# Scans of the last groups: x rows loaded inside the by-tile projection, row products one scan step later

## The chip, the cores and the metric

The kernel runs on one core of a Trainium2 chip. A core has five engines that run side by side, each through its own list of instructions, strictly in the order of that list: TensorE (PE, matrix products, with its weight loads shown as PEld), VectorE (DVE), ScalarE (ACT), GpSimd (POOL) and SyncE (SP), which here only issues DMA transfers. Engines wait for each other, and for transfers, on semaphores. An instruction that waits holds up all that stands behind it on its engine, and that goes for the transfers in SP's list too.

The metric is the time of one execution in microseconds (us), the median of several runs. A run with the profiler on leaves a trace, from which the profile is made; its times are counted from the start of the span.

## The reference

One inference step of a trunk with two layers over 1024 prompt tokens (one sequence) and 64 sample tokens (8 sequences of 8): a Mamba-2 SSD layer, then a layer of causal pooling. Each layer normalises x, modulates it, applies its branch and adds the result to x through a gate. Cut to the SSD branch, which is where the change lies:

```python
D_MODEL, D_INNER, N_HEADS, HEAD_DIM, N_GROUPS, D_STATE, CHUNK = 1024, 2048, 32, 64, 8, 128, 128

def ssd_branch(h, conv_prev, ssm_prev, w_in, conv_w, conv_b, dt_bias, a_log, d_skip, norm_g, w_out):
    zxbcdt = h @ w_in                                  # z, x/B/C and dt of every token
    conv = conv_b + sum(xp[:, k:k + L] * conv_w[k] for k in range(CONV_WIDTH))
    xbc_act = silu(conv)
    ...
    y, new_ssm = ssd_scan(xs, dt, A, Bm, Cm, ssm_prev) # chunks of 128 tokens, state passed on
    y = (y + d_skip[:, None] * xs).reshape(b, L, D_INNER)
    gated = (y * silu(z)).reshape(b, L, N_GROUPS, D_INNER // N_GROUPS)
    gated = gated * rsqrt(mean(gated * gated, axis=-1, keepdims=True) + EPS)
    gated = gated.reshape(b, L, D_INNER) * norm_g
    return gated @ w_out, new_conv, new_ssm
```

The eight groups are independent in the scan. The normalisation of `gated` goes over the 256 channels of one group, so a group's rows are final as soon as its own scan is done, and `gated @ w_out` can be added up over groups. x then becomes x + (1 + gate) * out.

## The kernel before

**Tiles.** Activations lie with channels on the 128 partitions and all 1088 tokens (1024 + 64) along the row. The tokens are worked in three pieces `CH` of 368, 368 and 352. Every matrix product is made in float32 out of halves: an activation is split into a high part (`gh`, `hh`, a rounding copy on ACT) and the rest (`gl`, `hl`, a subtraction on DVE), a weight likewise into `wh` and `wl`, and three matmuls (L184 high by high, L185 low activation, L186 low weight) replace one.

**The SSD layer.** `ssd_layer` goes through the eight groups. `scan_group(g)` is a generator that does one group's scan in 11 steps and leaves two more (the mean square with its rsqrt and the row products) as `rest`, which is run during the next group's scan. Beside each step the table `FILL` takes one to five pieces of other work out of `beside()`: first the projections of groups 1, 2, 3, 4 and 6, then the out-projection in parts. This other work is there to keep TensorE busy, since a scan is a chain of small operations over all engines.

**The projection by tile.** The last projection tile of all (group 6, fourth tile) doesn't run piece by piece but over the eight input tiles k one after the other, holding three accumulators (`ps`), so that each input tile's two buffers are given back as soon as it was used. Between its steps `next(self.prep)` loads and splits the rows for the first part of the out-projection: `op_stage` fetches a row tile `gr` from DRAM (`gyd`, L756), `op_split` makes `gh` (ACT, L761) and `gl` (DVE, L762). A part has four row tiles, and `op_part_load` has five steps. At the end the accumulators are evicted into `raw` by ACT (`proj_evict`, L424 and L426).

**The out-projection.** `op_units(p)` adds part p (four row tiles, of two groups) to all eight x tiles. `load_x` fetches an x tile (L1587), two tiles ahead (`XA = 2`), `op_evict` adds the product to it (DVE, L803, L806, L808), and the result goes to DRAM (`x1d`, L1612) until the next part. The very first tile (`op_first`, L786 to L791) does all the `gh` matmuls of all three pieces before any of `gl`.

**A scan's own operations**, as far as the text speaks of them. For each of eight chunks of 128 tokens: a load of decays `acb` from DRAM (L539; three tiles take turns), from which ACT makes the mask factors `M` (L571, L572), `ea` (L555) and `cd` (L591); transposes (`tr`, L563 and L566); a copy `Bt` (L583); a state sum `S` on PE (L605); the new state `h` (DVE, L610 and L614) and the rows `y` on PE (L626 from `M`, L630 from the state). For the samples: states `h0` are loaded (L528), read by PE (`Z`, L645), updated (DVE, L684) and stored (`hsT`, L686). When all rows are there they are multiplied by `z` (L721), squared (ACT, L722), summed (L723) and averaged with a matmul against ones (L727); the root goes through DRAM (`rsd`, L732) and comes back spread over all partitions (`rs`, L735). The row products then are two operations of DVE, each followed by its store:

```python
        for q in range(2):
            nc.vector.scalar_tensor_tensor(out=xs[q], in0=xs[q], scalar=..., in1=rst, op0=ALU.mult, op1=ALU.mult)  # L739
            if g < 7:
                nc.sync.dma_start(self.gyd[2 * g + q], xs[q])                                                     # L742
```

**Buffers.** `x`, `gr`, `gh`, `gl`, `h0`, `z`, `rs` and `xbc` all come out of one list of 30 buffers (`Slots`), handed out first in, first out: the n-th request gets the buffer that was given back n-th. So a request that moves ahead of another changes which buffer each later one gets, and what each must wait for.

**What sets the order.** The code above fixes which operations there are and what depends on what. The order of the instructions on each engine is then worked out by a scheduler with costs of its own, so a line that moves in the source may move other instructions too.

Of the kernel before, what the change touches and what calls it, by code (L numbers as in the profile page):

```python
# [28 lines left out]
XA = 2  # L29
# [70 lines left out]
class Build:  # L100
# [289 lines left out]
    def proj_group(self, G):  # L390

        for ii in range(4):
            w = self.stream_next()
            raw = self.proj_begin(G, ii)
            if (G["g"], ii) == (BESIDE[-1], 3):

                ps = [self.mm_tile() for _ in CH]
                for k in range(8):
                    for c, j in ((0, k), (1, k), (2, 0), (2, k)) if k == 1 else ((0, k), (1, k), (2, k))[:3 if k else 2]:
                        self.mm1(ps[c], w, j, self.hn[j], CH[c], j == 0, j == 7)  # L400
                    for j in (0, 1) if k == 1 else (k,) if k else ():
                        self.slots.free(*self.hn[j])
                    if k:
                        next(self.prep, None)
                    if k < 7:
                        yield
                for c in range(3):
                    self.proj_evict(G, ii, raw, ps[c], c, False)
                yield
                self.late = lambda: self.proj_end(G, ii, raw, True)  # L410
                return
            ada = self.ada_do(self.ada_plan[G["g"], ii]) if (G["g"], ii) in self.ada_plan else iter(())
            for c in range(3):
                ps = self.mm_tile()
                self.mm3(ps, w, self.hn, CH[c])
                self.proj_evict(G, ii, raw, ps, c)
                if c:
                    next(ada, None)
                yield
# [1101 lines left out]
    def ssd_layer(self):  # L1521
        nc, sl = self.nc, self.slots
        T, rest = {0: self.G[0]["out"]}, iter(())
        self.x = [None] * 8
        self.acts = [[] for _ in PARTS]
        self.prep = self.op_part_load(0, self.acts[0])
        self.fill = self.beside(T)
        for g in range(8):
            sc = self.scan_group(g, T[g])
            for i, n in enumerate(FILL[g]):  # L1530
                next(sc)
                for j in range(n):
                    next(self.fill)
                    if i in (0, 3) and j == 0:
                        next(rest, None)
                if i == 8 and g + 1 in self.G:
                    T[g + 1] = [sl.get("xbc") for _ in range(4)]
                    for t, d in zip(T[g + 1], self.xbd[g + 1]):
                        nc.sync.dma_start(t, d)
            rest = sc  # L1540
        self.prep = self.op_part_load(3, self.acts[3])
        self.out_unit()
        next(rest)
        for _ in range(2):
            next(self.fill)
        self.out_unit()
        for _ in rest:
            pass
# [39 lines left out]

    def op_units(self, p):

        for d in range(XA):
            self.load_x(p, d)
        for d in range(8):
            if d > 7:
                if (p, d) in self.ada_late:
                    for _ in self.ada_do(self.ada_late[p, d]):
                        pass
                    yield None
                continue
            self.load_x(p, d + XA)  # L1600
            if d % 2 == 0:
                ws = self.stream_pair()
            blk = self.ada_do(self.ada_late[p, d]) if (p, d) in self.ada_late else iter(())
            if p + d == 0:
                yield from self.op_first(0, self.x, d, ws[0], self.acts[p])
            for i, ch in enumerate(CH if p + d else ()):
                ins = self.op_unit(0, self.x, d, ws[d % 2], self.acts[p], ch)
                if i != 1:
                    next(blk, None)
                yield ins  # L1610
            if p < 2:
                self.nc.sync.dma_start(self.x1d[d], self.x[d])  # L1612
                self.slots.free(self.x[d])
# [264 lines left out]
```

## Time and profile before

| | |
|---|---|
| median of 3 runs | 1607.52 us (1605.69 to 1610.42) |
| the profiled execution | 1610.37 us, its span 1608.6 us |
| granted TensorE clock, mean | 0.996 |
| PE busy | 1579.8 us, 98% of the span |
| DVE, ACT, POOL busy | 1295.1, 792.3, 506.4 us |
| PE idle in the span | 28.8 us (1608.6 less 1579.8) |

The profiled execution is 2.85 us above the median of the three runs, so a sum made on its times is carried over to the median as a difference. TensorE is busy almost all of the time; what an edit of order can give or take is its idle time, which the profile names with the instruction that came late ("PE y L630 <- DVE h L610" reads: a matmul of line 630 waited for a DVE operation of line 610 on the tile h). In a timeline row the first number is the start, the second the duration, and a bracket at the end tells how long the engine had been idle before it and for whom. A row with "x3" stands for three instructions of that kind in a run. The changed lines act in the scans of groups 5, 6 and 7, some 690 to 930 us into the span.

### The profile page before, as it was taken

The numbers are of one execution on the slowest core, as the hardware profiler recorded it, in microseconds if no ns is written. First come the engines' busy times: TensorE is split into PE (matmuls) and PEld (weight loads), VectorE is DVE, ScalarE is ACT, GpSimd is POOL, SyncE is SP. The second block draws the span as 40 slices with busy tenths as digits, with TensorE's granted clock in tenths as the row PEclk, the third lists the DMA queues.
The fourth block names the chain that finished last, engine by engine and source line by source line (L and its number), as shares of the span: only waits on it lengthen the run. The fifth ranks groups of instructions, "written<-read, shape, count | busy, mean of one in ns | idle before, by whom it ended". The sixth has DMA issues, their size and how long they took to land.

```text
span 1608.6 us, 30632 instructions
## 1 busy us (share of the span) xinstructions
PE 1579.8 (98%) x11916; PEld 1506.0 (94%) x11916; DVE 1295.1 (81%) x2152; ACT 792.3 (49%) x1512; POOL 506.4 (31%) x558
## 2 busy tenths in 40 slices
PE   8999999999999999999999999999999999999997
PEld 6899999998888889888898899999999999999997
DVE  6974879778888888788889867998889776677886
ACT  6663344457676666674555437532232233333364
POOL 0133556512231313131212232275666630000241
PEclk9999999999999999999999999999999999999999
DMA  9422232355645554768998532132333279465783
GB/s 351 165 100 100 78 111 83 110 180 158 197 156 172 165 188 145 235 226 282 304 336 300 207 131 78 58 143 102 115 112 110 106 255 350 139 173 177 161 175 120
DMA packets 122305, 275.58 MB, mean 171 GB/s; under 512 B 18192, under 2 KB 59312, under 8 KB 122160
## 3 DMA queue, kind: packets, MB, share of 16 engines
q1 hardware_dynamic: 118128, 260.90, 47.2%
q0 software_dynamic: 4032, 12.72, 4.5%
q8 instruction: 94, 1.54, 0.4%
q14 instruction: 51, 0.42, 0.1%
HBM read 201.12 MB, written 70.23 MB: 169 GB/s over the span
## 4 chain that ended last, share of the span: by engine, by line
PE 79%; DVE 8%; DMA 5%; issue 4%; ACT 3%; POOL 1%; SPq 0%; DVEq 0%; ACTq 0%; POOLq 0%
PE st L1032 10%; PE st L1030 10%; PE st L1031 10%; PE mm L184 10%; PE mm L185 9%; PE mm L186 9%; PE op L1247 2%; PE op L1248 2%; PE op L1246 2%; PE y L626 2%; PE S L605 2%; PE y L630 2%; PE am L255 1%; PE tr L566 1%; DMA acb<-acd 1%
## 5 line engine op out<-in xcount | busy, mean ns | idle before, releaser
L1030 PE MATMUL st<-hh,w 128*128 128x272 f32 x832 | 240.3, 289 | 0.8 <-ACT w L176 0.8
L1032 PE MATMUL st<-hh,w 128*128 128x272 f32 x832 | 240.4, 289 | 0.4 <-DVE w L178 0.4
L1031 PE MATMUL st<-hl,w 128*128 128x272 f32 x832 | 240.0, 288 | 0.0
L1030 PE MATMUL st<-t,w 128*128 128x272 f32 x624 | 179.6, 288 | 0.0
L1032 PE MATMUL st<-t,w 128*128 128x272 f32 x624 | 179.5, 288 | 0.0
L1031 PE MATMUL st<-t,w 128*128 128x272 f32 x624 | 179.2, 287 | 0.0
L184 PE MATMUL mm<-hh,wh 128*128 128x368 f32 (+1 forms) x528 | 178.2, 338 | 0.0
L185 PE MATMUL mm<-hl,wh 128*128 128x368 f32 (+1 forms) x528 | 173.6, 329 | 0.0
L186 PE MATMUL mm<-hh,wl 128*128 128x368 f32 (+1 forms) x528 | 173.3, 328 | 0.0
L1030 PEld LDWEIGHTS st<-hh,w 128*128 128x128 f32 x832 | 156.8, 188 | 1.3 <-ACT w L176 1.3
L1032 PEld LDWEIGHTS st<-hh,w 128*128 128x128 f32 x832 | 156.4, 188 | 0.9 <-DVE w L178 0.9
L1031 PEld LDWEIGHTS st<-hl,w 128*128 128x128 f32 x832 | 156.7, 188 | 0.0
L613 POOL TENSOR_TENSOR hd<-h,cd 128x256 f32<-128x256 f32 x56 | 46.8, 836 | 322.6 <-DVE h L614 165.2
L176 ACT ACTIVATE w<-wr 128x512 fp32r<-128x512 f32 x104 | 64.9, 629 | 166.3 <-PE st L1032 137.4
L1247 PE MATMUL op<-b,w 128*128 128x272 f32 x448 | 128.9, 288 | 0.7 <-DVE b L1176 0.7
L1246 PE MATMUL op<-b,w 128*128 128x272 f32 x448 | 129.5, 289 | 0.0
L1248 PE MATMUL op<-b,w 128*128 128x272 f32 x448 | 128.9, 288 | 0.0
L184 PE MATMUL mm<-gh,wh 128*128 128x368 f32 (+1 forms) x372 | 125.6, 339 | 2.0 <-DVE x L803 1.9
L186 PE MATMUL mm<-gh,wl 128*128 128x368 f32 (+1 forms) x372 | 122.3, 329 | 0.0
L185 PE MATMUL mm<-gl,wh 128*128 128x368 f32 (+1 forms) x372 | 121.9, 328 | 0.1
L1030 PEld LDWEIGHTS st<-t,w 128*128 128x128 f32 x624 | 117.6, 189 | 0.1
L1032 PEld LDWEIGHTS st<-t,w 128*128 128x128 f32 x624 | 117.3, 188 | 0.0
(307 smaller groups left out, 4564.8 us busy)
## 6 DMA issues: line engine op xcount, KB each, us to landing
wr<-win SPq DMA_DIRECT2D x48, 512.0 KB, 6.0
acb<-acd SPq DMA_DIRECT2D x64, 256.0 KB, 4.6
wr<-pin SPq DMA_DIRECT2D x32, 512.0 KB, 3.8
wr<-pout SPq DMA_DIRECT2D x28, 512.0 KB, 4.7
x<-x1d SPq DMA_DIRECT2D x24, 544.0 KB, 5.7
x1d<-x SPq DMA_DIRECT2D x22, 544.0 KB, 4.7
wr<-pout POOLq DMA_DIRECT2D x20, 512.0 KB, 5.9
x<-xT SPq DMA_DIRECT2D x16, 544.0 KB, 7.3
```

Source lines behind the costliest of these rows:

```text
L176: self.nc.scalar.activation(hi, src, AF.Copy)
L184: nc.tensor.matmul(ps[:, :n], hi[:, k, :], ah[:, a:a + n], start=first, stop=False)
L185: nc.tensor.matmul(ps[:, :n], hi[:, k, :], al[:, a:a + n], start=False, stop=False)
L186: nc.tensor.matmul(ps[:, :n], lo[:, k, :], ah[:, a:a + n], start=False, stop=last)
L605: nc.tensor.matmul(S[:, 256 * i:256 * i + 256], Bt, xde.rearrange("p r q -> p (r q)"), start=True, stop=True)
L613: nc.gpsimd.tensor_tensor(out=hd, in0=h[-1], in1=cd.unsqueeze(2).to_broadcast([P, 4, 64]), op=ALU.mult)
L1030: nc.tensor.matmul(ps[c][:, :QUART], hi[:, k], xh[:, t], start=(k == 0), stop=False)
L1031: nc.tensor.matmul(ps[c][:, :QUART], hi[:, k], xl[:, t], start=False, stop=False)
L1032: nc.tensor.matmul(ps[c][:, :QUART], lo[:, k], xh[:, t], start=False, stop=(k == 3))
L1246: nc.tensor.matmul(ps[:, :QUART], hi[:, k], xh, start=k == 0, stop=False)
L1247: nc.tensor.matmul(ps[:, :QUART], hi[:, k], xl, start=False, stop=False)
L1248: nc.tensor.matmul(ps[:, :QUART], lo[:, k], xh, start=False, stop=k == 7)
```

## The change

```diff
@@ proj_group: the by-tile projection of the last tile
                         self.mm1(ps[c], w, j, self.hn[j], CH[c], j == 0, j == 7)
                     for j in (0, 1) if k == 1 else (k,) if k else ():
                         self.slots.free(*self.hn[j])
-                    if k:
+                    if k in (4, 5):
+                        self.load_x(0, k - 4)
+                    if 0 < k < 7:
                         next(self.prep, None)
                     if k < 7:
                         yield
                 for c in range(3):
                     self.proj_evict(G, ii, raw, ps[c], c, False)
+                next(self.prep, None)
                 yield
@@ ssd_layer
                 for j in range(n):
                     next(self.fill)
-                    if i in (0, 3) and j == 0:
+                    if i in (0, 3 + (g > 4)) and j == 0:
                         next(rest, None)
@@ op_units
-        for d in range(XA):
+        for d in range(XA if p else 0):
             self.load_x(p, d)
```

Three things are edited. First, the x tiles 0 and 1 of the out-projection's first part are requested at the steps k = 4 and 5 of the by-tile projection, each ahead of that step's gate load and split, and no more at the head of `op_units`. Second, the last call of `prep` in the projection stands behind its evictions. Third, in the scans of groups 5, 6 and 7 the second piece of `rest`, the row products of the group before (4, 5 and 6), is run at scan step 4 instead of 3.

The number and kinds of the instructions stay as they were. In the changed kernel the lines behind the first hunk are numbered three higher (L424 is L427, L739 is L742, L761 is L764, and so on). The order of the instructions differs only in the stretch named above. Three places:

ACT, at the end of the by-tile projection. `gh` are the gate halves of the first out-projection part, each from its loaded row `gr`; `raw<-mm` is the projection's eviction; `z<-xbc` is the square of the rows. The numbers behind a name count the tiles. Before:

```order
L761 ACTIVATE gh_139_8404<-gr_135_8387 128x1088
L761 ACTIVATE gh_142_8442<-gr_138_8402 128x1088
L362 ACTIVATE raw1106_8108<-raw1136_8306 128x1112
L761 ACTIVATE gh_144_8455<-gr_141_8440 128x1088
L424 ACTIVATE raw1145_8352<-mm1146_8355 128x368
L424 ACTIVATE raw1145_8352<-mm1147_8356 128x368
L141 ACTIVATE wh1153_8487<-wr1144_8350 128x1024
L424 ACTIVATE raw1145_8352<-mm1148_8357 128x288
L426 ACTIVATE raw1145_8352<-mm1148_8357 128x8x8
L722 ACTIVATE z_128_8214<-xbc_121_7586 128x1088
L359 ACTIVATE raw1200_8738<-raw1145_8352,cwh_263 128x1112
```

And after:

```order
L764 ACTIVATE gh_139_8404<-gr_135_8387 128x1088
L764 ACTIVATE gh_143_8444<-gr_138_8402 128x1088
L362 ACTIVATE raw1106_8108<-raw1136_8306 128x1112
L427 ACTIVATE raw1145_8352<-mm1146_8355 128x368
L427 ACTIVATE raw1145_8352<-mm1147_8356 128x368
L141 ACTIVATE wh1153_8487<-wr1144_8350 128x1024
L427 ACTIVATE raw1145_8352<-mm1148_8357 128x288
L429 ACTIVATE raw1145_8352<-mm1148_8357 128x8x8
L725 ACTIVATE z_128_8214<-xbc_121_7586 128x1088
L764 ACTIVATE gh_146_8459<-gr_142_8442 128x1088
L359 ACTIVATE raw1200_8738<-raw1145_8352,cwh_263 128x1112
```

The fourth gate half (gh_144 before, gh_146 after, of the same row) moved from ahead of the evictions to behind the square; its new buffer is the one that the sample state h0_126 gave back, and it waits for that state's store `hsT`.

DVE, at the row products L739 of group 4 (in group 5's scan). `x<-mm,gat,x` are evictions of the out-projection into an x tile, `h<-S` is the copy of the first state that PE waits for. Before:

```order
L803 SCALAR_TENSOR_TENSOR x_147_8483<-mm1178_8615,gat0_271,x_147_8483 128x368
L739 SCALAR_TENSOR_TENSOR xbc_120_7427<-xbc_120_7427,vec_193,rs_149_8553 128x1088
L803 SCALAR_TENSOR_TENSOR x_147_8483<-mm1179_8629,gat0_271,x_147_8483 128x288
L806 TENSOR_TENSOR gs1180_8643<-mm1179_8629,gat0_271 128x64
L610 COPY h1182_8649<-S1181_8646 128x256
L808 TENSOR_TENSOR x_147_8483<-x_147_8483,gs1180_8643 128x64
```

After, the products stand some thirty rows further down, together, in the next x tile but one:

```order
L806 SCALAR_TENSOR_TENSOR x_150_8574<-mm1227_8862,gat0_271,x_150_8574 128x368
L765 TENSOR_TENSOR gl_157_8879<-gr_152_8719,gh_156_8878 128x1088
L742 SCALAR_TENSOR_TENSOR xbc_120_7427<-xbc_120_7427,vec_193,rs_149_8553 128x1088
L742 SCALAR_TENSOR_TENSOR xbc_121_7586<-xbc_121_7586,vec_193,rs_149_8553 128x1088
L806 SCALAR_TENSOR_TENSOR x_150_8574<-mm1228_8886,gat0_271,x_150_8574 128x288
L809 TENSOR_TENSOR gs1229_8900<-mm1228_8886,gat0_271 128x64
```

So the pair left the place ahead of the state copy and now stands between two evictions.

SP, the transfers around the start of group 7's scan. `acb` are the scan's decays, `hsT` the store of the sample states of group 6, `x1d<-x` the store of an out-projected x tile, `x<-x1d` the load of one for the next part. Before:

```order
L714 DMA hpT<-h1435_10015 128x256
L119 DMA wr1470_10251<-wout 128x2x512
L1587 DMA x_201_10241<-x1d0_161 128x1088
L539 DMA acb1472_10267<-acd_72 128x4x128
L539 DMA acb1473_10269<-acd_72 128x4x128
L539 DMA acb1474_10271<-acd_72 128x4x128
L119 DMA wr1512_10461<-wout 128x2x512
L1612 DMA x1d6_167<-x_180_9812 128x1088
L1587 DMA x_203_10245<-x1d2_163 128x1088
L686 DMA hsT<-h0_188_9973 128x1024
L686 DMA hsT<-h0_189_9975 128x1024
L1587 DMA x_202_10243<-x1d1_162 128x1088
```

And after:

```order
L717 DMA hpT<-h1435_10015 128x256
L1590 DMA x_201_10241<-x1d0_161 128x1088
L119 DMA wr1470_10251<-wout 128x2x512
L1615 DMA x1d6_167<-x_180_9812 128x1088
L689 DMA hsT<-h0_189_9975 128x1024
L689 DMA hsT<-h0_188_9973 128x1024
L1590 DMA x_202_10243<-x1d1_162 128x1088
L1590 DMA x_203_10245<-x1d2_163 128x1088
L1615 DMA x1d7_168<-x_184_9928 128x1088
L542 DMA acb1472_10267<-acd_72 128x4x128
L542 DMA acb1473_10269<-acd_72 128x4x128
L542 DMA acb1474_10271<-acd_72 128x4x128
```

The three first loads of the new scan's decays moved behind two stores of states, two loads of x and the store x1d7.

## The prediction

> **What bounds the kernel now.** I read the page's first part, then the waits of TensorE in the stretch that the change reorders (690 to 930 us of the span), then 20 us slices of that stretch, and last the timelines around each wait.
>
> ```profile
> PE 1579.8 (98%) x11916; PEld 1506.0 (94%) x11916; DVE 1295.1 (81%) x2152; ACT 792.3 (49%) x1512; POOL 506.4 (31%) x558
> ```
>
> PE is busy 1579.8 of 1608.6 us, so 28.8 us of idle time is all that any reordering could win. No instruction is added or removed; only the idle time of PE can move. In the stretch it idles here:
>
> ```profile
> 710.00:730.00 20.00, 16.63 (x109) 14.63 (x102) 17.30 (x22) 11.79 (x17) 1.44 (x2) 1.00 0.87 309
> 730.00:750.00 20.00, 18.42 (x132) 17.22 (x132) 16.75 (x30) 9.54 (x20) 2.21 (x2) 1.00 0.80 269
> 750.00:770.00 20.00, 20.00 (x168) 18.12 (x165) 18.55 (x42) 11.96 (x33) 4.27 (x7) 1.00 0.95 330
> 870.00:890.00 20.00, 19.31 (x153) 18.00 (x152) 17.98 (x36) 10.87 (x31) 3.08 (x4) 1.00 0.90 306
> sum 240.00, PE 233.14 PEld 213.24 DVE 208.53 ACT 126.21 POOL 48.30; mean PE 19.43 PEld 17.77 DVE 17.38 ACT 10.52 POOL 4.03
> ```
>
> Busy times of PE, weight loads, DVE, ACT and POOL, then the clock (full) and the DMA share. Of 240 us PE idles 6.9: 3.4 in the first slice, 1.6 in the second, 0.7 around 880. The waits:
>
> ```profile
> PE mm L786 <- ACT raw L424: 1.9, 1, 1.9
> ...
> PE y L630 <- DVE h L610: 1.6, 1, 1.6
> PE S L605 <- ACT Bt L583: 1.0, 2, 0.7
> ```
>
> **Part 1, x0 and x1 loaded inside the by-tile projection.** The two loads take two turns of the slot list earlier, so the tiles after them shift. The fourth gate half gh (before: third in ACT's row ahead of the projection's first eviction) now gets the buffer that the sample states h0 leave, and that is free only when their store hsT has landed. x0, which used to get that buffer, gets an earlier one. First the stall ahead of the first out-projection tile:
>
> ```profile
> 716.95 1.09 ACT L761 ACTIVATE gh<-gr 128x1088 fp32r<-128x1088 f32 x1
> 717.95 0.82 ACT L424 ACTIVATE raw<-mm 128x368 f32<-128x368 f32 x2
> ...
> 721.30 1.31 ACT L359 ACTIVATE raw<-raw,cwh 128x1112 f32<-128x1112 f32 x1
> ```
> ```profile
> 718.46 0.43 PE L786 MATMUL mm<-gh,wh 128*128 128x368 f32 x1 [1.94 <-ACT raw L424]
> ...
> 721.18 0.41 PE L786 MATMUL mm<-gh,wh 128*128 128x368 f32 x1
> ...
> 723.24 0.50 PE L791 MATMUL mm<-gl,wh 128*128 128x368 f32 x2
> ```
>
> The split at 716.95 stands right ahead of the eviction for which PE waits. It goes behind z's square (which ends at 721.30), so the eviction starts at 716.95, 1.0 us earlier, and PE starts at 717.46: the stall falls from 1.94 to 0.94. The work between 718.46 and 721.18 then ends at 720.18, and six matmuls of the third gate half (half of the twelve between 721.18 and 723.24, 1.0 us) end at 721.18. There PE needs the fourth half. ACT is free for it at 721.30; the split takes 1.1 and needs the store:
>
> ```profile
> 712.24 0.94 SPq L1587 DMA_DIRECT2D x<-xT  x2
> 717.25 0.34 SPq L686 DMA_DIRECT2D hsT<-h  x1
> ```
> ```profile
> 722.50 0.82 SPq L1587 DMA_DIRECT2D x<-xT  x2
> ```
> ```profile
> hsT<-h SPq DMA_DIRECT2D x16, 512.0 KB, 2.7
> ```
>
> Before, x0's load stood at SP's head and went out at 722.50, when that store of 717.25 had landed: 5.25 us. The profile's median for such stores is 2.7, which would be 719.95, ahead of ACT. After, less goes out on the queue just ahead of it (two x loads were issued at 712.24; now it is one, the other having gone out a gate load earlier), so I take 721.8, nearer to 722.50, the row of this very store. The split then ends at 722.9 and PE idles 1.77 us at 721.18 (bounds: 1.3 with the store in time, 2.5 with a landing at 722.5).
>
> The Trainium skill, "DMA: Bandwidth & Descriptors", section "Anatomy of one DMA — SWDGE (gpsimd) path", gives about 2.0 us plus bytes over 436 GB/s for one DMA, stated for transfers of GpSimd; an estimate from it for these 512 KB is 3.2 us, a landing at 720.45, and part 1 would come out 0.5 us better. The row above says 5.25 with the DMA engines 87% busy, so the sum does not follow that estimate.
>
> The second stall was x0 itself:
>
> ```profile
> 728.95 1.53 DVE L803 SCALAR_TENSOR_TENSOR x<-mm,gat,x 128x368 f32<-128x368 f32 x3 [1.67 <-DMA x<-xT]
> ```
> ```profile
> 729.60 0.44 PE L184 MATMUL mm<-gh,wh 128*128 128x368 f32 x1 [1.31 <-DVE x L803]
> ```
>
> After, x0 is loaded at about 711, and no wait is left for it: the 1.31 us goes. ```profile
> DMA to landing us min/median/max: 5.3/6.1/8.6
> ```
>
> x1, which now waits for the other h0 store (issued about 1.8 us later on SP, landing some 1 to 2 us after the first), is loaded behind two other x loads; it was in hand early before and is needed only after mm1169 at about 728 and its 2.0 us of matmuls. An issue at about 724 lands at 730.1 by the median of line L1587's loads in the row above, and at 732.6 by their longest; DVE would then evict on time or some 2 us late. With two accumulators in flight PE may feel up to 1 us of that; I keep this in the upper bound and cost it at nothing in the sum.
>
> Part 1: 1.94 + 1.31 before, 0.94 + 1.77 after: a gain of 0.5 us (from 1.0 gained to 1.2 lost).
>
> **Part 2, the loop at the head of the out-projection runs over nothing for the first part.** It only takes away what part 1 did earlier, 0 us. The gate step moved behind the evictions issues nothing: part 0 has five steps, and the steps at k = 1 to 5 use them up in both versions. What moved that split is the slot.
>
> **Part 3, row products one scan step later in groups 5, 6 and 7's scans.**
>
> ```profile
> 730.11 0.32 SPq L735 DMA_DIRECT2D rs<-rsd  x1
> ```
> ```profile
> 737.26 1.35 DVE L739 SCALAR_TENSOR_TENSOR xbc<-xbc,vec,rs 128x1088 f32<-128x1088 f32 x1 [2.71 <-DMA rs<-rsd]
> ...
> 742.90 1.34 DVE L739 SCALAR_TENSOR_TENSOR xbc<-xbc,vec,rs 128x1088 f32<-128x1088 f32 x1
> ```
> ```profile
> 739.55 0.66 PE L630 MATMUL y<-ea,h 128*64 128x128 f32 x8 [1.58 <-DVE h L610]
> ```
>
> DVE waited 2.71 us for the broadcast rs, issued 7.1 us before, and the state copy L610 that PE needs stood behind it. With the product gone from there, DVE reaches L610 4.06 us earlier (2.71 + 1.35), far more than 1.58: the stall goes but for some 0.13 of ordinary handover: 1.45 us gained (1.0 to 1.6). The pair now stands at about 756, where 2.7 us of DVE work lands at once between two evictions. In the slice 750 to 770 DVE has 1.45 us free and PE none, so those 2.7 us come out of DVE's backlog, which is 4.06 us lighter than before: cost 0. What is late next: the two rows' stores and the h0 and z loads that take their buffers.
>
> ```profile
> h<-h0T SPq DMA_DIRECT2D x16, 512.0 KB, 8.9
> ```
> ```profile
> gyd<-xbc SPq DMA_DIRECT2D x2, 544.0 KB, 4.5
> ```
> ```profile
> 777.50 1.07 PE L645 MATMUL Z<-h,ctm 128*32 128x256 f32 x16
> ```
>
> Rows stored at 757 land at about 762 by the 4.5, and h0 is in at about 771 by the 8.9; its first reader on PE comes at 777.50. A margin of 6 us hides it; beyond that each us costs one.
>
> For group 6's products, in group 7's scan, the order shows more. The three first acb loads of the scan moved behind the store x1d7:
>
> ```profile
> 854.27 1.53 SPq L539 DMA_DIRECT2D acb<-acd  x3
> ...
> 867.34 0.33 SPq L1612 DMA_DIRECT2D x1d<-x  x1
> 867.76 0.39 SPq L539 DMA_DIRECT2D acb<-acd  x1
> ```
> ```profile
> 859.33 0.40 ACT L571 ACTIVATE M<-acb,tka 128x128 f32<-128x128 f32 x1 [1.41 <-DMA acb<-acd]
> ...
> 865.83 1.26 ACT L571 ACTIVATE M<-acb,tka 128x128 f32<-128x128 f32 x4
> ...
> 867.12 0.63 ACT L572 ACTIVATE M<-M 128x512 f32<-128x512 f32 x1
> ...
> 872.63 0.63 ACT L555 ACTIVATE ea<-acb 128x512 f32<-128x512 f32 x1 [1.38 <-DMA acb<-acd]
> ```
> ```profile
> 873.94 1.03 PE L605 MATMUL S<-xd,Bt 128*128 128x256 f32 x4
> ...
> 884.78 0.70 PE L605 MATMUL S<-xd,Bt 128*128 128x256 f32 x2 [0.69 <-ACT Bt L583]
> ```
> ```profile
> 879.88 1.35 DVE L739 SCALAR_TENSOR_TENSOR xbc<-xbc,vec,rs 128x1088 f32<-128x1088 f32 x1 [1.22 <-DMA rs<-rsd]
> ```
>
> They go out behind 867.34, at 867.7 instead of 854.27, and arrive at about 872.6 (the load issued at 867.76 was read at 872.63). ACT then needs 1.2 for the first M, 0.5 for ea and 0.6 for the exponential: 874.9, and DVE 0.7 for the product: 875.6. PE, now with one S ahead of it instead of two, wants that M at about 874.85 (873.94 + 0.3 + 0.6): a new stall of 0.8. The second Bt stands on ACT behind some 2.9 us more (second M 1.2, two of 0.5, a quarter of the third M, the copy), 877.8, against 877.2 on PE: 0.6. Some 0.3 follow at the next S. Gone are the 0.69 and 0.32 that PE waited for Bt, since L739 with its 1.22 no longer stands ahead on DVE. So 1.7 − 1.0 = 0.7, I take 0.8 lost. Bounds: 1.0 gained (no new stall, the 13 us of lead was slack) and 3 lost (each of three fronts 1 us later, in a ring of three tiles).
>
> For group 5's products the pair moves the same way with little wait at its place; one eviction wait is there:
>
> ```profile
> 796.87 0.43 PE L184 MATMUL mm<-gh,wh 128*128 128x368 f32 x1 [0.59 <-DVE x L803]
> ```
>
> DVE's rows around it change places, some earlier, some later; cost 0, from 0.6 gained to 1.1 lost (the sum of squares now stands behind a weight split of 1.1).
>
> **The sum.** −0.5 − 1.45 + 0.8 + 0 = −1.15 us. Against the profiled execution's 1610.37 that is 1609.2; this run lies 2.85 us above the median of the three, 1607.52, so the forecast for a median is 1606.4.
>
> **The rivals.**
> - *All stalls go.* The store lands by 720 (its 2.7 us median), x1 isn't late and group 7's new places are covered: −1.0 − 1.6 − 0.6 − 1.0 = −4.2, 1603.3. For it: the median; against it: the 5.25 at this place and a DMA share of 0.80 to 0.95.  Chance 0.17; it ends at the edge of what counts as faster.
> - *Slower: group 7's scan starves.* Its tiles acb are three; a load takes about 5 us here and its three readers on ACT 2.3 per front, so a start 13 us later leaves no reserve. If each of the first four fronts makes PE wait 1.5 us, that is 6 − 1.0; with −1.95 of parts 1 and 3, +3.0: 1610.5. It ends slower when x1d7's store goes out after 867.3, us for us: at 870 the sum is +6, 1613.5. Against it: PE's first need lies 7 us behind 867.7. Chance 0.2.
> - *The change only moves the wait.* The store lands at 722.5 or later and x1 late: part 1 loses 1.2 and only the 1.45 is left, less 0.8: +0.5, 1608.0. Chance 0.15.
>
> **How the numbers follow.** My forecast's own case has 0.48. The predicted time is its 1606.4. The range goes from 1602.8 (all stalls gone, 0.5 for the medians' own scatter) to 1611.8 (the starving case up to +4). A change of 0.3% is 4.8 us, about what a measurement tells from none: faster than 1602.7 takes a part of the first rival and some scatter, 0.12; slower than 1612.3 most of the starving case and unseen transfers, 0.18; the rest, 0.70, is the same.
>
> **What would show it.** In the profile after: the wait ahead of L789 (before L786) at 1.0 instead of 1.94; a new wait of 1.3 to 2.5 some 3.7 us later for ACT's gh; none for x0 at the next tile; no wait of PE for the state copy at 739; DVE's product pair near 756 with no wait for rs; acb loads at 867 to 869 and waits of PE for M and Bt at 875 to 886 of 1 to 2 us together. The prediction is wrong if PE's idle time in 690 to 930 falls below 3 us or rises above 11, or if the difference lies outside this stretch.

## The result

The changed kernel took 1610.85 us (median of 21 runs, 1606.50 to 1613.83), the kernel before in the same sessions 1606.65 us (21 runs, 1601.74 to 1611.09): a ratio of 1.0027, with a 95% interval of 1.0019 to 1.0036, or 4.2 us slower. Measured a second time it was 1.0032 (1.0020 to 1.0043). The forecast was 1.15 us faster. The first measure lies just under the 0.3% that I called the same, the second just over it. The sign is wrong, and since both intervals are clear of 1, it is no scatter.

The profile of the changed kernel (span 1611.4 us) hardly differs in its totals:

```profile
PE 1580.3 (98%) x11916; PEld 1503.6 (93%) x11916; DVE 1296.0 (80%) x2152; ACT 792.4 (49%) x1512; POOL 507.3 (31%) x558
```

These are the waits of PE in 690 to 990 us of the changed kernel (total, times, longest, in us):

```profile
PE S L608 <- ACT Bt L586: 1.7, 3, 0.9
PE ms L730 <- DVE z L726: 1.2, 2, 0.7
PE mm L789 <- ACT gh L764: 1.0, 1, 1.0
PE mm L789 <- ACT raw L427: 1.0, 1, 1.0
PE y L629 <- DVE M L580: 0.9, 1, 0.9
```

The waits on which the prediction turned have changed the way it said: the wait for the eviction fell from 1.94 to 1.0, a new one of 1.0 for the fourth gate half came in, and those for x0 and for the state copy are gone. The wait for M is new. And yet this kernel is slower. Slices by 20 us show where (PE, weight loads, DVE, ACT, POOL, clock, DMA share):

```profile
710.00:730.00 20.00, 18.01 (x116) 16.06 (x115) 19.32 (x22) 14.52 (x22) 2.42 (x2) 1.00 0.85 305
730.00:750.00 20.00, 20.00 (x155) 19.29 (x155) 16.48 (x33) 10.67 (x23) 1.61 (x2) 1.00 0.90 292
...
870.00:890.00 20.00, 18.27 (x144) 16.29 (x142) 15.30 (x34) 14.37 (x43) 2.65 (x4) 1.00 0.93 274
890.00:910.00 20.00, 19.12 (x151) 16.07 (x149) 16.72 (x37) 10.81 (x32) 3.52 (x7) 1.00 0.85 320
910.00:930.00 20.00, 19.26 (x137) 16.96 (x137) 16.83 (x28) 7.40 (x9) 7.49 (x6) 1.00 0.35 116
```

The last two of these slices before:

```profile
890.00:910.00 20.00, 19.68 (x171) 17.60 (x170) 16.86 (x39) 9.77 (x28) 5.95 (x8) 1.00 0.66 246
910.00:930.00 20.00, 20.00 (x134) 18.68 (x134) 16.74 (x29) 6.50 (x7) 2.88 (x5) 1.00 0.35 118
```

PE idles 3 us less in the first two slices than in the profile before, and 2.3 us more in the last three.

To compare many profiles I used a mark that each has: the matmul of the mean square (ms, L727 before, L730 after), once per group. Its starts for groups 6 and 7, first in the kernel before, then in the changed one:

```profile
866.75 0.67 PE L727 MATMUL ms<-z,ones 128*32 128x272 f32 x8
919.22 0.67 PE L727 MATMUL ms<-z,ones 128*32 128x272 f32 x8
```
```profile
867.07 0.67 PE L730 MATMUL ms<-z,ones 128*32 128x272 f32 x8
923.90 0.67 PE L730 MATMUL ms<-z,ones 128*32 128x272 f32 x8 [0.74 <-DVE z L726]
```

From mark to mark that is 52.47 us before and 56.83 after. The table has these distances for every profile taken, kernels in the order in which they come below (us; "4 to 5" holds the places of x0 and of the row products of group 4, "6 to 7" the scan of group 7):

| profile | 4 to 5 | 5 to 6 | 6 to 7 |
|---|---|---|---|
| before (the prediction's) | 75.22 | 67.67 | 52.47 |
| before, second profile | 71.74 | 67.67 | 53.33 |
| before, third profile | 72.20 | 67.67 | 53.32 |
| changed | 72.10 | 67.67 | 56.83 |
| changed, second profile | 72.11 | 67.68 | 55.96 |
| x loads early alone | 75.63 | 67.68 | 55.34 |
| x loads early alone, second | 75.27 | 67.68 | 57.63 |
| row products later alone | 72.47 | 67.67 | 52.27 |
| row products later alone, second | 71.98 | 67.67 | 52.52 |
| changed, group 6's products back | 72.10 | 67.66 | 57.80 |
| changed, acb from ScalarE's queue | 72.11 | 69.62 | 52.73 |
| changed, acb from ScalarE's queue, second | 72.32 | 72.46 | 52.16 |
| changed, acb earlier on SyncE | 72.10 | 67.66 | 53.18 |

### The profile page after: what moved, and what is told of

It reads as the page before. It is cut to its first block, busy times and chain, and to the rows that moved or that the text cites. A ratio compares the mean times of both kernels' runs of the same rounds, so it can differ in the third digit from the quotient of the medians.

```text
span 1611.4 us, 30632 instructions
## 1 busy us (share of the span) xinstructions
PE 1580.3 (98%) x11916; PEld 1503.6 (93%) x11916; DVE 1296.0 (80%) x2152; ACT 792.4 (49%) x1512; POOL 507.3 (31%) x558
## 4 chain that ended last, share of the span: by engine, by line
PE 81%; DVE 6%; DMA 6%; issue 4%; ACT 3%; POOL 0%; SPq 0%; DVEq 0%; ACTq 0%; POOLq 0%
PE st L1035 10%; PE st L1033 10%; PE st L1034 10%; PE mm L184 9%; PE mm L186 9%; PE mm L185 9%; PE op L1250 3%; PE op L1251 3%; PE op L1249 3%; DMA acb<-acd 2%; PE y L629 2%; PE S L608 2%; PE y L633 2%; DMA rsd<-z 1%; PE am L255 1%
```

## The experiments

My first theory after the result: the early stalls were won, and more was lost in group 7's scan, because its first acb loads stand late on SP. The rivals: group 6's row products at their new place, or the shifted buffers themselves.

**One part alone: the x loads.** Hunks one and two without hunk three:

```diff
-                    if i in (0, 3 + (g > 4)) and j == 0:
+                    if i in (0, 3) and j == 0:
```

> Hunks one and two alone: x0 and x1 loaded inside the by-tile projection, row products where they were. By the order the state copy that PE waited for at 739 now stands ahead of group 4's row products, and the three first decay loads (acb) of group 7 stand early on SP, as before the change. Theory (the loss of the changed kernel is the late acb loads): all three stalls of 718 to 740 shrink, as they did with the change (-3.0 us by 809 us in its profile), and group 7's scan is as before: 2 to 3.5 us faster than before. Rival (the moved x loads and slots cost in the later scans by themselves): 1 to 4 us slower than before, with the loss in 870 to 930.

Measured: 1613.99 us against 1608.00 of before, a ratio of 1.0036 (1.0022 to 1.0050): by its value slower than the whole change (the intervals overlap), and the theory's 2 to 3.5 us of gain is refuted. This part alone is 3 us slow from mark 4 to 5 and 2 to 4 us from 6 to 7.

**The other part alone: the row products.** Hunk three on the kernel before:

```diff
-                    if i in (0, 3) and j == 0:
+                    if i in (0, 3 + (g > 4)) and j == 0:
```

> Hunk three alone: row products of groups 4, 5 and 6 one scan step later, x loads as before. By the order group 4's first row product still stands ahead of the state copy on DVE, and group 7's acb loads stand early. Theory: the stalls of 718, 729 and 739 us stay and nothing is lost in group 7: within 1 us of before. Rival (row products of group 6 a step later are what group 7's scan suffers from): 2 to 4 us slower, lost in 870 to 930.

Measured: 1606.59 us against 1608.00, ratio 0.9988 (0.9975 to 1.0001), the same time, as the theory expected. But its reason was wrong. The stalls of 729 and 739 were to stay, and in the profile only 0.34 us of the first is left and nothing of the second, though the order there is that of the kernel before. That pointed at the profile of before itself.

**Group 6's row products back at step 3.** In the changed kernel:

```diff
-                    if i in (0, 3 + (g > 4)) and j == 0:
+                    if i in (0, 3 + (4 < g < 7)) and j == 0:
```

> The changed kernel with group 6's row products (in group 7's scan) back at scan step 3; groups 4 and 5's stay later. By the order the acb loads of group 7 stay late on SP. Theory (late acb loads): as slow as the changed kernel, 3 to 5 us slower than before. Rival (group 6's later row products are the loss): 2 to 3.5 us faster than before.

Measured: 1612.26 us against 1608.00, ratio 1.0020 (1.0005 to 1.0036), 3.2 us slower by the ratio, and 57.80 from mark 6 to 7. With group 6's products at their old place and the acb loads late, the loss is there in full; the products' new place in group 7 is not its cause.

**The acb loads from another queue.** In the changed kernel:

```diff
-                nc.sync.dma_start(t, self.acd[...])
+                (nc.scalar if g == 7 and c < 3 else nc.sync).dma_start(t, self.acd[...])
```

> The changed kernel, with the three first acb loads of group 7's scan issued from ScalarE's queue instead of SyncE's, where they stood behind two state stores, two x loads and an x store. Everything else as in the changed kernel, so the row products of group 6 stay one step later. Theory (late acb loads are the loss): the waits of PE for M and Bt in 874 to 900 go, 4 us faster than the changed kernel and 2 to 3.5 us faster than before. Rival (the later row products, or the slots): no more than 1 us faster than the changed kernel.

Measured: 1611.33 us against 1608.00, ratio 1.0025 (1.0005 to 1.0044), runs from 1605.84 to 1619.00. Unclear as a time. By the marks, 6 to 7 is back at 52.73, but 5 to 6 has grown from 67.67 to 69.62. A second measurement, beside the changed kernel:

> The changed kernel with the three first acb loads of group 7 issued from ScalarE's queue, beside the changed kernel on the same chip. If the late acb loads are the loss, at least 2 us faster than the changed kernel here; if not, within 1 us of it.

Measured: 1612.22 us against 1606.15, ratio 1.0035 (1.0022 to 1.0049), no faster than the changed kernel beside it (1611.28). The expectation failed, and the trace of this second run tells why. ScalarE first, then PE:

```profile
844.53 0.21 ACT L594 ACTIVATE cd<-acb 128x4 f32<-128x4 f32 x1 [4.98 <-DMA acb<-acd]
848.67 0.21 ACT L594 ACTIVATE cd<-acb 128x4 f32<-128x4 f32 x1 [3.77 <-DMA acb<-acd]
```
```profile
851.51 1.44 PE L648 MATMUL Z<-h,ctm 128*32 128x256 f32 x16 [3.46 <-issue]
```

With the loads on its own queue the scheduler put two small readers of acb (`cd`) so early in ScalarE's row that ScalarE stood 8.75 us waiting for the transfers, and all behind it came late, up to PE at Z. The cure of 6 to 7 (52.16) was paid for in 5 to 6 (72.46). This edit moved more than the one wait and couldn't decide by its time.

**The kernel before, twice more.** No edit; the question was whether the stalls of the prediction belong to the kernel.

> The kernel before, profiled once more. The first profile of it lay 2.85 us above the median of its runs, and two of the three stalls that the prediction counted as gain (1.31 us for x0 at 729 and 1.58 us for the state copy behind the row products at 739) add up to 2.89. Theory A (those two are one slow draw of the transfers, not a property of the kernel): they are gone or below 0.5 us each here, while the wait for the eviction (1.94) stays at over 1. Rival: both are there again, at over 1 us each.

> The same, a third profile of the kernel before: theory A expects that at least one of the two waits is below 0.5 us in each of the new profiles, the rival that both are over 1 us in both.

Measured: 1610.45 and 1607.37 us in one execution each. The waits of PE in 690 to 990 us, second profile, then third:

```profile
PE mm L786 <- ACT raw L424: 2.4, 1, 2.4
PE S L605 <- ACT Bt L583: 1.7, 1, 1.7
PE Z L645 <- PE y L630: 0.3, 1, 0.3
PE mm L184 <- DVE x L803: 0.2, 1, 0.2
```
```profile
PE S L605 <- ACT Bt L583: 1.9, 2, 1.5
PE mm L786 <- ACT raw L424: 1.9, 1, 1.9
PE mm L184 <- DVE x L803: 0.3, 1, 0.3
PE Z L645 <- PE y L630: 0.3, 1, 0.3
PE y L630 <- DVE h L610: 0.3, 1, 0.3
```

Theory A holds: these two waits are not in every execution of the kernel. The wait for the eviction is there each time (1.94, 2.4, 1.9), so it belongs to the order. The wait of 1.31 for x0 and that of 1.58 for the state copy are there in the first profile only; 0 and 0.27 are what is left of the latter. They hang on when two transfers land. Whether chance made these late in the first profile, or the chip that it ran on, is not shown. For the row products' rs, issue and first use on DVE in the third profile:

```profile
731.02 0.32 SPq L735 DMA_DIRECT2D rs<-rsd  x1
```
```profile
737.03 1.35 DVE L739 SCALAR_TENSOR_TENSOR xbc<-xbc,vec,rs 128x1088 f32<-128x1088 f32 x1 [1.39 <-DMA rs<-rsd]
```

Here 6.0 us from issue to use, 7.15 in the first profile: that one microsecond, with the later x0 ahead of it, was the stall. The mark distance 4 to 5 says the same: 75.22 once, 71.74 and 72.20 since, and 72.47 and 71.98 in the two profiles with hunk three alone, whose order up to that place is the same.

Two more things stand in these profiles. The second one (1610.45) is as long as the first (1610.37) without either wait, so it is by chance that the two waits add up to the first one's distance from the median. And a stall of the same kind is in each of the three, only in another group's scan: in the second profile PE waits 1.96 us at 590.74 and in the third 1.82 us at 442.00 for the state copy, behind a row product that had waited 2.93 and 2.79 us for rs.

```profile
590.74 0.66 PE L630 MATMUL y<-ea,h 128*64 128x128 f32 x8 [1.96 <-DVE h L610]
```

**The changed kernel, once more.**

> The changed kernel, profiled and timed again. What belongs to the new order must come again: the wait of 1.0 us for the fourth gate half, 0.5 us ahead of the mean square at 799, and over 2 us of waits for M and Bt in the scan of group 7. 3 to 5 us slower than before. A rival (the loss in group 7 was a slow draw) expects under 1 us there.

Measured: 1611.28 us against 1606.15, ratio 1.0032 (1.0020 to 1.0043). The waits of its profile:

```profile
PE ms L730 <- DVE z L726: 1.2, 2, 0.7
PE mm L789 <- ACT gh L764: 1.0, 1, 1.0
PE y L629 <- DVE M L580: 0.9, 1, 0.9
PE mm L789 <- ACT raw L427: 0.6, 1, 0.6
PE S L608 <- ACT Bt L586: 0.6, 2, 0.5
```

The new waits came again (gate half 1.0, M 0.94, mean square 0.5 and 0.74), only those for Bt were smaller. The waits for M and Bt sum to 1.6, less than the 2 that I expected; the distance from mark 6 to 7 is 55.96, still 2.6 us above the two newer profiles of before.

**The acb loads earlier on the same queue.** In the changed kernel the first two of group 7's loads are written at the end of group 6's scan, so that they stand on SP right behind group 6's last store of states (hpT):

```diff
             for i, n in enumerate(FILL[g]):
                 next(sc)
+                if i == 10 and g == 6:
+                    self.acb7 = [self.gs.tile([P, 4, 128], F32, tag="acb", bufs=3, ...) for _ in range(2)]
+                    for c, q in enumerate(self.acb7):
+                        nc.sync.dma_start(q, self.acd[28:32, 128 * c:128 * c + 128]...)
...
         def load_ac(c):
             if c < 8:
+                if g == 7 and c < 2:
+                    acbs[c] = self.acb7[c]
+                    return
```

> The changed kernel, with the first two acb loads of group 7 written at the end of group 6's scan, so that they stand on SyncE ahead of the state stores, x loads and x store; no other queue is used, and nothing of ScalarE's consumers is placed early. Theory (those late loads cost about 3.4 us in 862 to 952): the stretch 862 to 952 takes no longer than in the kernel before, the waits for M and Bt there sum to under 1.5 us, and the time is 3 to 4 us below the changed kernel, that is within 1 us of the kernel before. Rival (the loss there has another cause, such as the row products of group 6 one step later): within 1.5 us of the changed kernel.

Measured: 1607.86 us against 1608.44 of before, ratio 1.0002 (0.9992 to 1.0012), where the changed kernel was 1.0027 and 1.0032. The expectations of the theory came in: the time is that of the kernel before, the mark distance 6 to 7 is 53.18 against 53.33 and 53.32 of before, and the waits for Bt there sum to 1.4. SP's issue, then the marks of groups 6 and 7, then the waits:

```profile
843.70 1.83 SPq L1541 DMA_DIRECT2D acb<-acd  x2
```
```profile
861.66 0.67 PE L733 MATMUL ms<-z,ones 128*32 128x272 f32 x8
914.84 0.67 PE L733 MATMUL ms<-z,ones 128*32 128x272 f32 x8
```
```profile
PE S L611 <- ACT Bt L589: 1.4, 2, 1.1
PE mm L792 <- ACT gh L767: 1.0, 1, 1.0
PE ms L733 <- DVE z L729: 0.5, 1, 0.5
```

The wait for M and the second one for ms are gone; the loads go out 18 us ahead of the mark instead of on it (867.01 in the changed kernel, its mark at 867.07). So the late acb loads are shown to be the cause of the loss.

What they cost is not waiting alone. PE's row from mark 6 to 7, in the third profile of before, in the changed kernel and with the loads early (length, then busy time of PE with its matmuls, and so on as above):

```profile
866.25:919.57 53.32, 51.38 (x410) 46.65 (x409) 46.81 (x96) 25.97 (x66) 11.89 (x16) 1.00 0.68 238
867.07:923.90 56.83, 53.48 (x409) 46.14 (x408) 46.68 (x94) 32.11 (x82) 13.66 (x16) 1.00 0.73 247
861.66:914.84 53.18, 51.73 (x409) 46.62 (x409) 46.17 (x94) 28.00 (x70) 13.56 (x16) 1.00 0.75 264
```

For the same matmuls at the full clock PE is busy 2.1 us longer in the changed kernel and idle 1.4 us longer; in its second profile (busy 53.53) it is 2.2 and 0.5. The profile models the ends of matmuls, so this split is rough.

**Hunk three alone, again.**

> Hunk three alone, timed once more, since it was 1.9 us below the kernel before with an interval that just held 1. If the later row products of groups 5 and 6 do help by themselves, again 1 to 3 us faster; if that was scatter, within 1 us of the kernel before.

Measured: 1609.11 us against 1608.44, ratio 1.0003 (0.9991 to 1.0015): the 1.9 us of the first time were scatter. Hunk three alone does nothing to the time.

**The x loads alone, a second profile.**

> Hunks one and two alone, profiled once more. It was 5.8 us slower than before, and its profile showed the weight load for S at 779 landing late behind a load of z that stood on SyncE until a store of x had landed (6.6 us). If that is its order and not a slow draw, the wait of SyncE for that store and a wait of PE of over 1 us behind it come again between 770 and 785, and another of over 1.5 us near 900.

Measured: 1614.53 us in one execution. The wait of SP for the store came again:

```profile
SPq L526 <- DMA x1d<-x: 6.5, 1, 6.5
```

and so did ScalarE's wait for the weights that stand behind it on SP:

```profile
775.44 1.06 ACT L141 ACTIVATE wh<-wr 128x1024 fp32r<-128x1024 f32 x1 [9.10 <-DMA wr<-wout]
```

(6.6 and 9.45 in its first profile; 2.3 and 0.84 in the third profile of before.) PE felt it as expected. The wait for Bt, whose copy stands right behind these weights on ScalarE, came again (1.84 us at 779.61 in the first profile, 1.49 here), and so did one of 1.2 us for an eviction ahead of mark 5:

```profile
776.40 0.26 ACT L586 ACTIVATE Bt<-tr 128x128 f32<-128x128 f32 x1
```
```profile
776.71 0.70 PE L608 MATMUL S<-xd,Bt 128*128 128x256 f32 x2 [1.49 <-ACT Bt L586]
799.25 0.44 PE L184 MATMUL mm<-gh,wh 128*128 128x368 f32 x1 [1.20 <-DVE x L806]
```

With the x rows requested earlier, the z rows of group 5 get a buffer from which a store is still going out; SP stands 6.5 us at that load, and the weights behind it are late. The two waits of PE (3.05 and 2.69 us together, where the changed kernel has 0.50) are most of the 3 us from mark 4 to 5. An edit that takes only SP's wait away wasn't tried. Hunk three hides it: with both, the distance is 72.10.

The 2 to 4 us from mark 6 to 7 have another source, since the acb loads of the scan's start stand early here. The wait near 900 that the expectation names is there in both profiles (2.37 and 2.31 us): on ScalarE a small reader of a later acb (`es`) now stands ahead of a Bt copy and waits 3.4 us for its load. Behind this wait the granted clock is at half for about 3.4 us in both; the third profile of before has only 0.40 there and the full clock. In the first profile, ScalarE, PE, and PE's slice (the clock is the third number from the end):

```profile
900.04 0.26 ACT L562 ACTIVATE es<-acb 128x32 f32<-128x32 f32 x1 [3.40 <-DMA acb<-acd]
900.20 0.26 ACT L586 ACTIVATE Bt<-tr 128x128 f32<-128x128 f32 x1
```
```profile
900.51 0.70 PE L608 MATMUL S<-xd,Bt 128*128 128x256 f32 x2 [2.37 <-ACT Bt L586]
```
```profile
902.00:906.00 4.00, 4.00 (x34) 3.67 (x29) 3.98 (x7) 3.46 (x11) 2.19 (x5) 0.57 1.04 407
```

No version that beats the kernel before was found.

## Why the prediction was wrong

- **What bounds the kernel, and the bound on the gain.** The place is right: PE stays at 98%, and what changed lies in the stretch named. But "only the idle time of PE can move" is wrong. PE's idle time from 690 to 930 us is 6.2 and 4.9 us in the two profiles of the changed kernel, against 6.9, 4.9 and 4.9 in three of before; what grew is the busy time of the same matmuls in group 7's scan, by about 2 us. Nearly all the signs that the prediction named came in, and yet the kernel is slower.
- **Part 1, the wait for the eviction (1.94 to 0.94).** Right: 0.99 and 0.65 in the two profiles of the changed kernel, 1.9 to 2.4 in three of before. It varies more than that elsewhere: 1.26 and 1.89 with hunk three alone, 0.2 to 0.9 in five further profiles with the x loads moved, and 1.93 in a sixth.
- **Part 1, the new wait for the fourth gate half (1.77, from 1.3 to 2.5).** The mechanism is right in part, the size too large: 1.00 and 1.04, below the lower bound, and its limit is not the store.

```profile
723.61 1.11 ACT L725 ACTIVATE z<-xbc 128x1088 f32<-128x1088 f32 x1 [1.13 <-DVE xbc L724]
724.63 1.09 ACT L764 ACTIVATE gh<-gr 128x1088 fp32r<-128x1088 f32 x1
725.63 1.30 ACT L359 ACTIVATE raw<-raw,cwh 128x1112 f32<-128x1112 f32 x1
```

The split runs on ScalarE without a gap behind the square, so the store had landed; the store went out at 720.53 at the earliest, and landed within 4.1 us. I had chosen the 5.25 us of one row over the 2.7 of the median. The estimate of 3.2 us, from the Trainium skill, "DMA: Bandwidth & Descriptors", section "Anatomy of one DMA — SWDGE (gpsimd) path" (stated there for transfers of GpSimd), agrees with this bound; the run doesn't show more than the bound.
- **Part 1, x0 (1.31 gained), and part 3, the state copy (1.45 gained).** This is the step that failed first. Both waits vanished, but they were not there to be won: of the first, two further profiles of before have nothing, of the second 0 and 0.27, and from mark 4 to 5 the changed kernel takes 72.1 us against 71.7 and 72.2. With the loss of group 7 taken back (the acb loads early), the ratio is 1.0002 (0.9992 to 1.0012); the 1.95 us that parts 1 and 3 were to win are not there. The stall for the state copy comes up in one group's scan or another, so taking it away in group 5's wins it only when it falls there. I carried the gain over to the median as a difference, as if every run had these waits. That they add up to 2.89, and the execution lay 2.85 us above the median, was luck: the second profile of before lay as high without them.
- **Part 3, group 7 (0.8 lost, from 1.0 gained to 3 lost).** The first waits are right, the size is not: this term makes the change slower. Measured from mark 6 to 7: 2.6 and 3.5 us against the newer profiles of before, and 2.8 to 3.7 of it came back with the loads early. The first wait, for M, is as worked out (0.8; 0.94 measured), that for the second Bt too (0.6; 0.46). Three things are missing in the sum. The chain goes on: another 0.34 and 0.88 for Bt in the first profile. The mean square of group 7 waits 0.74 for DVE. And PE's order was cut finer: scan rows that stood in one piece now stand between pieces of the out-projection, presumably since the scheduler, too, saw the loads late. I count 17 entries from scan work into projection matmuls between 868 and 934 us, 11 before, 10 with the loads early. Of the 4.4 us by which the first profile's distance grew, named waits make 2.35 (3.36 less 1.01); the rest is the longer busy time of PE's matmuls (51.46 to 53.48). I put it down to these cuts, which no run measures by themselves; with the loads early both the order and the busy time (51.73) are nearly those of before. I had also counted on winning the 1.0 us of the old waits for Bt.
- **Group 5's row products at nothing.** The wait of 0.59 near 797 (0.2 and 0.3 in the other profiles of before) gave way to one of 0.50 ahead of the mean square: nothing, as costed, near enough.
- **The rivals.** The slower one named the right place and queue. It needed 1.5 us at each of four fronts; what came is 0.3 to 0.9 at four places and the cut order.
- **The sum.** With −0.9 for the eviction, +1.0 for the gate half, 0 for x0 and the state copy, and +2.6 to +3.5 for group 7, the terms give about +2.7 to +3.6, against +4.2 and +5.1 measured. About 1 us is not located; from mark 3 to 4, mostly ahead of the change, the profiles scatter by more than that (75.0 to 78.7).

## What to carry to other kernels

A stall that waits for a transfer can be a draw; before its removal is counted as a gain, take a second profile of the same kernel and see whether the stall is there again. How far the profiled execution lies from the median doesn't tell: the second one here lay as high and had its stall elsewhere. And a cut into PE's order can cost busy time that no list of waits shows. When an edit shifts a first-in-first-out list of buffers or the scheduler's order, read the in-order queue of transfers in the changed order first: a load that moves behind a store whose data isn't ready costs the whole wait, and all its readers with it. What one part costs alone says little where the parts change each other's order: alone, these two cost 6 us and nothing, and together 4.

## What the runs showed of the hardware

- Where no transfer and no moved order makes PE wait longer, an execution repeats almost to the digit: from mark 5 to 6 eleven of thirteen profiles, of six kernels on several chips, have 67.66 to 67.68 us. The distances ahead of the change, from mark 0 to 3, vary by up to 3.8 us each with the same order.
- A part of that variation is the granted clock. Between 40 and 1590 us of the thirteen profiles it falls to 0.50 eleven times, for 3.3 to 3.5 us each, at the end of a wait of PE of 1.73 to 3.46 us or within 2 us behind it. Seven other waits of 1.75 to 2.42 us were not followed by it, and none shorter than 1.73 was. By these numbers one such fall costs PE an estimated 1.7 us. The runs show it too: of the 35 runs of the kernel before that were timed beside the x loads alone, the eleven with a mean clock of 0.997 took 1606.5 us on average, the seven with 0.994 took 1611.5. How much of the scatter of some 8 us between runs of one kernel the clock makes, and how much the transfers, was not separated.
- The same broadcast of a row (rs, 544 KB) took 7.15, 5.4 and 6.0 us from issue to use in the three profiles of the kernel before.
